# A two-layer hybrid block in float32: where the tiles begin in SBUF

## The chip, the cores and the metric

The kernel runs on one core of a Trainium2 chip. The metric is the device time of one execution in microseconds; the runs of the kernel before are given as a median with their lowest and highest. One further execution was taken with the hardware profiler, and all times of engines and instructions below are from that one.

## The reference

Two layers, each of a feed-forward half step, a mixer with three branches, and a second feed-forward half step, on 256 tokens of width 1024, in float32:

```python
for l in range(2):
    x = x + 0.5 * swiglu(rms_norm(x, ffn1_norm[l]), ffn1_w_gate[l], ffn1_w_up[l], ffn1_w_down[l])
    x = x + hybrid_mixer(rms_norm(x, mix_norm[l]), w_in[l], ..., w_branch[l], w_out[l])
    x = x + 0.5 * swiglu(rms_norm(x, ffn2_norm[l]), ffn2_w_gate[l], ffn2_w_up[l], ffn2_w_down[l])
```

swiglu(x) is (silu(x @ w_gate) * (x @ w_up)) @ w_down with 2816 hidden columns. hybrid_mixer projects its input with w_in and has three branches: a gated linear recurrence, a dilated window attention with 12 heads, and a chunked delta rule with 8 heads (a chain of small triangular solves). Their outputs go through w_branch, are gated, added, and go through w_out.

## The kernel before, in words

**The big matmuls.** Everything is kept transposed: features on the 128 partitions, the 256 tokens in the columns. A product with a weight matrix is a sum over blocks of 128 x 128 weights. Each float32 product is made of three products in the type float32r: a weight block w is split into wh (rounded) and wl (the rest), an activation into xh and xl, and wh xh, wh xl and wl xh are added up in PSUM. Two helpers issue them. In `stationary` the weight block is the stationary operand, loaded into TensorE by LDWEIGHTS, and the activation the moving one, 256 columns; this is nearly all of the kernel. In `moving`, used by the attention projections (kinds ak, aq, av), the activation is the stationary operand and the weight tile the moving one. Both call `pump` between matmuls, which may let another piece of work (a task) issue its instructions in between.

**The weights.** They lie in HBM in the order of use. `load_group` fetches one group of up to 1024 columns (512 KB) into one of the six tiles raw0 to raw5 through SyncE's queue; `convert` makes wh and wl of it, by ScalarE (rarely VectorE) and VectorE, in five tiles each of 1024 columns. A 128-column slice of such a tile is 512 bytes per partition.

**The small work.** Norms, gates, convolutions, the recurrence, the attention and the delta rule run as tasks (generators) on VectorE, ScalarE, GpSimd and, with small float32 matmuls into the PSUM tiles sm, on TensorE. Activations xh and xl live in 60 places s0 to s59 of 256 columns (1024 bytes per partition); larger ones in the arena, tiny ones in the tile tiny.

**What sets the order.** The whole order of instructions is fixed when the program is built. `Engine._cost` puts a price in ns on every instruction, `Prog.count` adds it to the planned clock of its engine, and `pump` issues a step of a task as soon as the planned clock of TensorE (`now`) has passed the planned end of what the step needs. The price of a float32r matmul is in `Engine._cost`: 0.46 ns for each moving column, so 117.8 ns for 256. A price does nothing on the chip; it decides behind which big matmul a step is issued. `move` chooses between ScalarE and VectorE by the same planned clocks.

**Where the tiles lie.** The pool sb places its tiles in SBUF one after another, in the order in which `Prog.__init__` declares them, each at a multiple of 32 bytes. cst (8280 bytes per partition) begins 128 bytes past a multiple of 1024, prm (1760) follows, then raw, wh, wl, X, zr, ssq, which all have sizes that are multiples of 1024 bytes and begin 960 bytes past such a multiple; eps_n and half (32 bytes each) fill the 64 bytes up to the next multiple, at which tiny begins, and so the arena and the places s behind it. Blocks within the arena begin at multiples of 256 bytes.

Of the kernel before, what the change touches and what calls it, by code (L numbers as in the profile page):

```python
# [10 lines left out]
F32 = mybir.dt.float32  # L11
# [6 lines left out]
P = 128  # L18
# [21 lines left out]
KEEP, KEEP2 = 3072, 2048  # L40
ARENA_COLS = 14336
NSLOT = 60
SPARE = 4
SLACK = (800.0, 1500.0, 1500.0, 1500.0, 1500.0, 600.0)
URGENT = 2
# [54 lines left out]
def flat_chunks():  # L100
    return [c for layer in all_jobs() for jobs in layer for job in jobs for c in job[2]]


def group_chunks(chunks):
    groups, cur, cols = [], [], 0
    for c in chunks:
        w = c[3] * c[5]
        if cur and cols + w > GROUP_COLS:
            groups.append((cur, cols))
            cur, cols = [], 0  # L110
        cur.append(c)
        cols += w
    groups.append((cur, cols))
    return groups
# [60 lines left out]
class Arena:  # L175
    def __init__(self, pr, ap, unit):
        self.pr, self.ap, self.unit = pr, ap, unit
        self.n = ap.shape[1] // unit
        self.busy = [False] * self.n
        self.stamp = [0.0] * self.n  # L180
        self.peak = 0
# [123 lines left out]
def _free(ap):  # L305
    n = 1
    for x in ap.shape[1:]:
        n *= x
    return n


class Engine:
# [16 lines left out]
    def _cost(self, name, a, k):  # L329
        key = self._key  # L330
        if key == "pe":
            lhsT = k["lhsT"] if name == "matmul" else a[1]
            rhs = k["rhs"] if name == "matmul" else a[2]
            n, m = _free(rhs), _free(lhsT)
            if lhsT.dtype == F32R:
                return max(0.46 * n, 0.83 * m)
            if name == "transpose":
                return 0.84 * max(n, m)
            if m <= 32 and lhsT.shape[0] <= 32:
                return 40.0  # L340
            if m <= 64 and lhsT.shape[0] <= 64 and n <= 64:
                return 100.0
            return 1.7 * max(n, m)
        n = _free(a[0])
        if name == "tensor_reduce":
            n = _free(a[1])
        if key == "a":
            c = 93 + 0.833 * n
            for x in ("scale", "bias", "accum_out"):
                c += 93 * (not isinstance(k.get(x, 0.0), float) and x in k)  # L350
            func = a[2] if name == "activation" else None
            sets = TABLES.get(func)
            if sets and self._pr.table not in sets:
                self._pr.table = sets[0]
                c += 1283
            return c
        if key == "g":
            return (330 + 160 * n) if k.get("op") == ALU.pow else 350 + 0.6 * n
        if name == "reciprocal":
            return 68 + 6.3 * n  # L360
        fast = name in ("tensor_copy", "tensor_scalar") and a[1].space != PSUM
        c = 68 + (0.52 if fast else 1.04) * n
        if name in ("scalar_tensor_tensor", "tensor_scalar") and not isinstance(a[2], float):
            c += 60
        if k.get("accum_out") is not None:
            c += 60
        return c
# [5 lines left out]
class Prog:  # L373
    def __init__(self, ctx, tc, io):
        self.tc, self.nc, self.io = tc, tc.nc, io
        nc = self.nc
        self.clock = {"pe": 0.0, "v": 0.0, "a": 0.0, "g": 0.0}
        self.table = None
        self.cur = self.main = Task(None, 0.0, 0)
        self.step, self.used = set(), {}  # L380
        self.tasks = []
        self.pe, self.v = Engine(self, "pe", nc.tensor), Engine(self, "v", nc.vector)
        self.a, self.g = Engine(self, "a", nc.scalar), Engine(self, "g", nc.gpsimd)
        sb = ctx.enter_context(tc.tile_pool(name="sb", bufs=1))
        ps = ctx.enter_context(tc.tile_pool(name="ps", bufs=1, space=PSUM))
        dr = ctx.enter_context(tc.tile_pool(name="dr", bufs=1, space=bass.MemoryType.DRAM))
        self.cst = sb.tile([P, CST["_n"]], F32, name="cst")
        self.prm = sb.tile([P, L * PRM["_n"]], F32, name="prm")
        self.raw = [sb.tile([P, GROUP_COLS], F32, name=f"raw{i}") for i in range(NRAW)]
        self.wh = [sb.tile([P, 1024], F32R, name=f"wh{i}") for i in range(NCONV)]  # L390
        self.wl = [sb.tile([P, 1024], F32R, name=f"wl{i}") for i in range(NCONV)]
        self.X = sb.tile([P, KD, T], F32, name="X")
        self.zr = sb.tile([P, T], F32, name="zr")
        self.ssq = sb.tile([P, T], F32, name="ssq")
        self.eps_n = sb.tile([P, 1], F32, name="eps_n")
        self.half = sb.tile([P, 8], F32, name="half")
        self.tiny_t = sb.tile([P, 1024], F32, name="tiny")
        self.ar_t = sb.tile([P, ARENA_COLS], F32, name="arena")
        self.tiny = Arena(self, self.tiny_t, 8)
        self.slots = Slots(self, sb, NSLOT)  # L400
        self.ar = Arena(self, self.ar_t, 64)
        self.big = Banks(self, [ps.tile([P, 512], F32, name=f"big{i}") for i in range(NBIG)])
        self.sm = Banks(self, [ps.tile([P, 512], F32, name=f"sm{i}") for i in range(8 - NBIG)])
        self.gdram = [dr.tile([16, P], F32, name=f"gd{l}") for l in range(L)]
        self.rdram = [[dr.tile([P, 64], F32, name=f"rd{l}_{i}") for i in range(4)] for l in range(L)]
        self.rc = [self.tiny.get(16).ap for _ in range(L)]
        self.ea = [self.tiny.get(8) for _ in range(L)]
        self.qg = [self.tiny.get(6) for _ in range(L)]
        self.groups = group_chunks(flat_chunks())
        self.chunk_at = []  # L410
        off = 0
        self.goff = []
        for gi, (cs, cols) in enumerate(self.groups):
            self.goff.append(off)
            c0 = 0
            for c in cs:
                self.chunk_at.append((c, gi, c0, c[3] * c[5]))
                c0 += c[3] * c[5]
            off += P * cols
        self.unread = [len(cs) for cs, _ in self.groups]  # L420
        self.cursor = 0
        self.dma_next = 0
        self.dma_clock = 0.0
        self.raw_t = {}
        self.conv_t = {}
        self.conv_next = 0
        self.when = {}
        self.ops = {}
        self.prepared = set()
        self.nsq = None  # L430
        self.npair = 4
# [111 lines left out]
    def get(self, cols):  # L543
        b = None
        if cols == T:
            b = self.slots.get(F32, SPARE)
        return b or self.ar.get(cols, self.keep())
# [1157 lines left out]
```

## Time and profile before

| | |
|---|---|
| runs of the kernel before | median 1630.62 us of 3 (1622.04 to 1631.97) |
| the profiled execution, its own time | 1627.63 us |
| its span, first to last instruction | 1625.4 us |
| mean granted clock of TensorE | 0.994 |
| TensorE matmuls busy | 1602.4 us |
| VectorE, ScalarE, GpSimd busy | 1159.2, 936.7, 139.3 us |
| read from HBM | 275.49 MB, 170 GB/s over the span |

The span is 2.2 us shorter than the execution's own time. In rows, PE is TensorE's matmuls, PEld its weight loads, DVE is VectorE, ACT ScalarE, POOL GpSimd. Nearly all instructions are issued from one line, that of the wrapper in class Engine (L323 before), so groups are told apart by the tiles: `big<-s,wh` is a matmul into a PSUM tile big with the moving operand s and the stationary operand wh; `128*128` is its rows and stationary columns, `128x256` what it writes; buffer numbers are left out. Matmuls are pipelined: a row's time in us reaches into the next row's, and what one matmul costs in a stream is the distance between starts.

### The profile page before, as it was taken

What the parts mean: (1) busy time and instruction counts of PE and PEld (TensorE: products, weight loads), DVE (VectorE), ACT (ScalarE), POOL (GpSimd) and SP (SyncE); (2) the same over time, 40 slices, a digit from 0 to 9 for tenths busy, and PEclk for the clock granted to TensorE, in tenths of its full rate; (3) what the DMA queues carried; (4) which work ended last, traced back from release to release, by engine and by line L of the source; (5) the groups of instructions that cost most, each with busy time, mean ns of one, the idle gap of its engine ahead of it and who ended that gap; (6) DMA issues with size and microseconds to landing.
All of it is one profiled execution on the core that took longest, in us unless ns stands there. A gap on an engine that the chain in (4) does not pass through costs nothing. (4 is left out here: it accounts for less than half of the span.)

```text
span 1625.4 us, 34428 instructions
## 1 busy us (share of the span) xinstructions
PE 1602.4 (99%) x13952; PEld 1560.0 (96%) x13952; DVE 1159.2 (71%) x2172; ACT 936.7 (58%) x1643; POOL 139.3 (9%) x280
## 2 busy tenths in 40 slices
PE   9999999999999999999999999999999999999999
PEld 8999999989988999999999999999898899999999
DVE  8666588987973667666566656989878756676653
ACT  7544456878854546444454445568887555554442
POOL 0000000345002000000000000003540120000000
PEclk9999999999998999999999999999999999999999
DMA  8655656544343565555555555656443345655562
GB/s 304 186 187 179 193 179 194 164 162 133 120 129 107 163 204 184 187 188 178 188 192 183 182 185 185 195 176 182 139 140 122 123 131 189 190 184 185 181 188 86
DMA packets 84942, 279.04 MB, mean 172 GB/s; under 512 B 10256, under 2 KB 15664, under 8 KB 84784
## 3 DMA queue, kind: packets, MB, share of 16 engines
q1 hardware_dynamic: 84784, 276.85, 53.7%
q8 instruction: 109, 1.79, 0.4%
q14 instruction: 49, 0.40, 0.1%
HBM read 275.49 MB, written 1.33 MB: 170 GB/s over the span
## 5 line engine op out<-in xcount | busy, mean ns | idle before, releaser
L323 PE MATMUL big<-s,wh 128*128 128x256 f32 (+1 forms) x7520 | 1346.3, 281 | 7.0 <-DVE s L323 6.0
L323 PEld LDWEIGHTS big<-s,wh 128*128 128x128 f32 (+1 forms) x7520 | 1151.0, 188 | 17.4 <-DVE s L323 6.8
L323 PE MATMUL big<-s,wl 128*128 128x256 f32 (+1 forms) x3760 | 1053.6, 280 | 0.0
L323 DVE TENSOR_TENSOR wl<-raw,wh 128x1024 fp32r<-128x1024 f32 (+3 forms) x523 | 620.8, 1187 | 248.4 <-ACT wh L323 245.2
L323 ACT ACTIVATE wh<-raw 128x1024 fp32r<-128x1024 f32 (+4 forms) x497 | 509.1, 1025 | 361.8 <-PE big L323 168.8
L323 PEld LDWEIGHTS big<-s,wl 128*128 128x128 f32 (+1 forms) x3760 | 705.3, 188 | 2.8 <-issue 1.8
L323 ACT ACTIVATE s<-s 128x256 fp32r<-128x256 f32 (+1 forms) x213 | 85.2, 413 | 116.6 <-DVE s L323 116.0
L323 POOL TENSOR_TENSOR tiny<-tiny,half 128x4 f32<-128x4 f32 (+1 forms) x28 | 38.6, 1378 | 1102.0 <-DVE tiny L323 1083.9
L323 PE MATMUL sm<-arena 128*128 128x128 f32 (+7 forms) x1440 | 114.0, 238 | 9.7 <-DVE arena L323 6.9
L323 PEld LDWEIGHTS sm<-arena 32*32 32x32 f32 (+5 forms) x1440 | 85.8, 138 | 30.2 <-issue 9.3
L323 PE MATMUL big<-wh,s 128*128 128x256 f32 x576 | 110.2, 287 | 0.0
L323 POOL TENSOR_TENSOR arena<-arena 128x60 f32<-128x60 f32 (+14 forms) x240 | 98.6, 411 | 62.6 <-DMA arena<-rd 44.7
L323 DVE TENSOR_TENSOR s<-s,s 128x256 fp32r<-128x256 f32 (+1 forms) x181 | 75.7, 422 | 36.5 <-ACT s L323 36.1
L323 PEld LDWEIGHTS big<-wh,s 128*128 128x128 f32 x576 | 89.6, 189 | 1.2
L323 DVE SCALAR_TENSOR_TENSOR s<-big,prm,s 128x255 f32<-128x255 f32 (+2 forms) x183 | 85.6, 477 | 6.6 <-ACT s L323 5.3
L323 DVE TENSOR_TENSOR arena<-big,zr 128x512 f32<-128x512 f32 x88 | 60.9, 692 | 34.8 <-PE big L323 34.5
L323 PE MATMUL big<-wl,s 128*128 128x256 f32 x288 | 82.1, 285 | 0.0
L323 ACT ACT_TABLE_LOAD x63 | 80.8, 1283 | 1.7 <-PEq L1697 0.7
L323 ACT ACTIVATE arena<-sm 128x128 f32<-128x128 f32 (+6 forms) x152 | 48.8, 323 | 37.6 <-PE sm L323 35.1
L323 ACT ACTIVATE s<-big 128x256 f32<-128x256 f32 x53 | 20.2, 382 | 62.1 <-PE big L323 62.1
L323 PEld LDWEIGHTS big<-wl,s 128*128 128x128 f32 x288 | 54.5, 189 | 0.4
L323 ACT ACTIVATE s<-big,prm 128x256 f32<-128x256 f32 x53 | 26.5, 499 | 45.2 <-PE big L323 45.0
(110 smaller groups left out, 772.3 us busy)
## 6 DMA issues: line engine op xcount, KB each, us to landing
raw<-wts SPq DMA_DIRECT2D x435, 512.0 KB, 3.7
raw<-wts SPq DMA_DIRECT2D x64, 448.0 KB, 3.6
raw<-wts SPq DMA_DIRECT2D x16, 384.0 KB, 3.1
arena<-rd SPq DMA_DIRECT2D x8, 512.0 KB
arena<-rgw SPq DMA_DIRECT2D x4, 512.0 KB, 5.2
arena<-gd SPq DMA_DIRECT2D x16, 128.0 KB, 4.7
X<-x SPq DMA_DIRECT2D x4, 256.0 KB, 4.9
raw<-wts SPq DMA_DIRECT2D x4, 256.0 KB, 3.2
```

Of the source, the lines that this page charges most:

```text
L323: r = f(*a, **k)
```

## The change

The constants tile eps_n and the tile half are declared right behind prm, and behind them a tile pad of 252 columns (1008 bytes) that nothing uses. eps_n and half now lie at 960 and 992 bytes past a multiple of 1024, the pad begins on the next multiple's place, and raw0 begins on a multiple of 1024; wh, wl, X, zr, ssq, tiny, the arena and the places s follow, all of them on multiples. In the built program raw0 goes from byte 26,560 to 27,648, wh0 from 51,136 to 52,224, s0 from 163,840 to 164,864. The second edit is the planner's price of a float32r matmul, 0.445 instead of 0.46 ns for a column.

```diff
@@ -40,6 +40,7 @@
 NSLOT = 60
+PAD = 252
 SPARE = 4
@@ -333,7 +334,7 @@
             if lhsT.dtype == F32R:
-                return max(0.46 * n, 0.83 * m)
+                return max(0.445 * n, 0.83 * m)
@@ -386,14 +387,15 @@
         self.cst = sb.tile([P, CST["_n"]], F32, name="cst")
         self.prm = sb.tile([P, L * PRM["_n"]], F32, name="prm")
+        self.eps_n = sb.tile([P, 1], F32, name="eps_n")
+        self.half = sb.tile([P, 8], F32, name="half")
+        sb.tile([P, PAD], F32, name="pad")
         self.raw = [sb.tile([P, GROUP_COLS], F32, name=f"raw{i}") for i in range(NRAW)]
         self.wh = [sb.tile([P, 1024], F32R, name=f"wh{i}") for i in range(NCONV)]
         self.wl = [sb.tile([P, 1024], F32R, name=f"wl{i}") for i in range(NCONV)]
         self.X = sb.tile([P, KD, T], F32, name="X")
         self.zr = sb.tile([P, T], F32, name="zr")
         self.ssq = sb.tile([P, T], F32, name="ssq")
-        self.eps_n = sb.tile([P, 1], F32, name="eps_n")
-        self.half = sb.tile([P, 8], F32, name="half")
         self.tiny_t = sb.tile([P, 1024], F32, name="tiny")
```

The new price moves steps of tasks to other places between the big matmuls. Of TensorE's 12,467 rows in the built program some 305 stand elsewhere; the big matmuls keep their order. The numbers behind the names in the next rows count the buffers in the order in which they are made and differ between the two programs; only the kinds of tiles and the shapes are to be compared.

The first place is TensorE at the end of the first feed-forward half step, where the small matmul for the next norm (sm from ssq) is issued. Before:

```order
L323 MATMUL big_91<-s_1708,wh_77 128x256
L323 MATMUL big_91<-s_1709,wh_77 128x256
L323 MATMUL sm_95<-ssq,cst 128x256
L323 MATMUL big_91<-s_1708,wl_82 128x256
L323 MATMUL big_91<-s_1789,wh_77 128x256
```

and now:

```order
L324 MATMUL big_92<-s_1710,wh_80 128x256
L324 MATMUL big_92<-s_1711,wh_80 128x256
L324 MATMUL big_92<-s_1710,wl_85 128x256
L324 MATMUL sm_96<-ssq,cst 128x256
L324 MATMUL big_92<-s_1791,wh_80 128x256
```

The small matmul stands one big matmul later; in the long feed-forward parts there are only such places. The second is TensorE in the attention projections of the first layer, among which the first pair of heads of the delta rule starts its chain of small products (sm from arena, 32x16, sixteen of them in a step). Before:

```order
L323 MATMUL big_92<-wh_77,s_2420 128x256
L323 MATMUL sm_95<-arena 32x16 x16
L323 MATMUL big_92<-wh_77,s_2450 128x256
L323 MATMUL big_92<-wl_82,s_2450 128x256
L323 MATMUL big_92<-wh_77,s_2451 128x256
L323 MATMUL big_92<-wh_73,s_2479 128x256
L323 MATMUL big_92<-wl_78,s_2479 128x256
L323 MATMUL sm_96<-arena 32x16 x16
```

and now, 69 rows further on:

```order
L324 MATMUL big_91<-wh_79,s_2403 128x256
L324 MATMUL sm_96<-arena 32x16 x16
L324 MATMUL big_91<-wh_79,s_2431 128x256
L324 MATMUL big_91<-wl_84,s_2431 128x256
L324 MATMUL big_91<-wh_79,s_2432 128x256
L324 MATMUL big_91<-wh_79,s_2455 128x256
L324 MATMUL big_91<-wl_84,s_2455 128x256
L324 MATMUL big_91<-wh_79,s_2456 128x256
L324 MATMUL big_91<-wh_80,s_2493 128x256
L324 MATMUL big_91<-wl_85,s_2493 128x256
L324 MATMUL sm_97<-arena 32x16 x16
```

Between the two steps stood five big matmuls and now stand eight; the chain starts later among the big matmuls.

## Rows read from the trace of the kernel before

**Rows 1.** The page's busy time by engine (share of the span, instructions), and the last link of the chain that ended last in order of time (start us, us, what).

```profile
PE 1602.4 (99%) x13952; PEld 1560.0 (96%) x13952; DVE 1159.2 (71%) x2172; ACT 936.7 (58%) x1643; POOL 139.3 (9%) x280
...
1438.51 183.51 PE big L323 x1558
```

**Rows 2.** The largest of TensorE's waits: who waited for whom, us in total, times, longest.

```profile
PE sm L323 <- DVE arena L323: 8.6, 8, 2.2
```

**Rows 3.** The page's groups of instructions that are big matmuls: line, engine, operation, tiles and count, then busy us, mean ns of one, idle time before them.

```profile
L323 PE MATMUL big<-s,wh 128*128 128x256 f32 (+1 forms) x7520 | 1346.3, 281 | 7.0 <-DVE s L323 6.0
L323 PE MATMUL big<-s,wl 128*128 128x256 f32 (+1 forms) x3760 | 1053.6, 280 | 0.0
L323 PE MATMUL big<-wh,s 128*128 128x256 f32 x576 | 110.2, 287 | 0.0
L323 PE MATMUL big<-wl,s 128*128 128x256 f32 x288 | 82.1, 285 | 0.0
```

**Rows 4.** TensorE in order of time at 700 us (start us, us, engine, line, instruction and count): the first and the last wl of four triples of two wh and one wl each.

```profile
700.08 0.28 PE L323 MATMUL big<-s,wl 128*128 128x256 f32 x1
...
701.49 0.28 PE L323 MATMUL big<-s,wl 128*128 128x256 f32 x1
```

**Rows 5.** The same view: what stands ahead of the stretch from 540 us, four triples in it at 600 us (first and last wl), and what ends it.

```profile
539.95 0.60 PE L323 MATMUL sm<-cst,arena 128*128 128x128 f32 x4
...
600.01 0.28 PE L323 MATMUL big<-s,wl 128*128 128x256 f32 x1
...
601.37 0.28 PE L323 MATMUL big<-s,wl 128*128 128x256 f32 x1
...
634.99 0.59 PE L323 MATMUL sm<-ssq,cst 128*128 128x256 f32 x2
```

**Rows 6.** Busy time by stretch (from:to and its length in us; busy us and instructions of each engine; granted clock, share of the DMA engines, GB/s): first of the instructions that write or read a big tile alone, then of all.

```profile
16.00:290.00 274.00, 270.51 (x2284) 269.06 (x2282) 44.92 (x88) 9.19 (x19) 1.00 0.61 196
290.00:325.00 35.00, 31.19 (x251) 30.22 (x252) 12.32 (x27) 3.28 (x7) 1.00 0.53 165
410.00:540.00 130.00, 87.22 (x662) 80.27 (x662) 13.51 (x30) 6.34 (x17) 0.95 0.38 119
540.00:635.00 95.00, 94.37 (x827) 93.84 (x826) 9.29 (x22) 5.05 (x14) 1.00 0.61 196
635.00:1098.00 463.00, 459.30 (x3879) 457.30 (x3877) 63.45 (x118) 9.19 (x19) 1.00 0.58 185
1098.00:1133.00 35.00, 31.08 (x250) 30.11 (x251) 12.95 (x28) 3.27 (x7) 1.00 0.61 180
1218.00:1345.00 127.00, 94.29 (x707) 86.08 (x708) 12.68 (x29) 7.69 (x19) 1.00 0.40 126
1345.00:1626.00 281.00, 276.68 (x2342) 275.87 (x2340) 27.48 (x51) 4.61 (x12) 1.00 0.55 172
...
16.00:290.00 274.00, 273.83 (x2309) 272.08 (x2308) 203.40 (x369) 150.12 (x226) 1.01 (x1) 1.00 0.61 196
290.00:540.00 250.00, 241.23 (x2237) 224.00 (x2236) 190.21 (x478) 174.60 (x385) 68.45 (x137) 0.97 0.43 133
635.00:1098.00 463.00, 462.68 (x3907) 460.65 (x3906) 321.14 (x487) 241.74 (x355) 1.01 (x1) 1.00 0.58 185
1098.00:1345.00 247.00, 240.76 (x2284) 224.82 (x2283) 192.03 (x478) 177.88 (x391) 68.60 (x137) 1.00 0.45 140
```

**Rows 7.** A stretch with a lower granted clock (columns as in rows 6), and TensorE in order of time around it.

```profile
367.20:367.90 0.70, 0.70 (x6) 0.70 (x5) 0.70 (x5) 0.70 (x4) 0.00 (x0) 0.50 0.38 146
...
367.38 0.41 PE L323 MATMUL big<-wl,s 128*128 128x256 f32 x1
367.59 0.63 PE L323 MATMUL big<-wh,s 128*128 128x256 f32 x2
```

**Rows 8.** TensorE in order of time in two runs of the moving form: the first and last wl of one with 12 triples of matmuls between them, and of one with 15.

```profile
358.46 0.28 PE L323 MATMUL big<-wl,s 128*128 128x256 f32 x1
...
362.70 0.28 PE L323 MATMUL big<-wl,s 128*128 128x256 f32 x1
...
394.98 0.28 PE L323 MATMUL big<-wl,s 128*128 128x256 f32 x1
...
400.08 0.28 PE L323 MATMUL big<-wl,s 128*128 128x256 f32 x1
```

**Rows 9.** TensorE in order of time: float32 matmuls of 256 columns, several in a row (each is one pass of two).

```profile
289.70 0.81 PE L323 MATMUL sm<-s,arena 128*128 128x256 f32 x3
...
298.04 1.02 PE L323 MATMUL sm<-s,arena 128*128 128x256 f32 x4
...
1009.74 0.59 PE L323 MATMUL sm<-ssq,cst 128*128 128x256 f32 x2
```

**Rows 10.** Groups by form: VectorE additions and ScalarE activations of 128x256 with operands in ssq, X and the places s (count, busy us, mean ns of one, idle before).

```profile
L323 DVE TENSOR_TENSOR s<-s,s 128x256 f32<-128x256 f32 x62 | 25.8, 421 | 0.4
L323 DVE TENSOR_TENSOR ssq<-ssq,s 128x256 f32<-128x256 f32 x39 | 16.3, 418 | 0.2
L323 ACT ACTIVATE s<-s 128x256 f32<-128x256 f32 x85 | 32.4, 409 | 1.3 <-DVE s L323 0.8
L323 ACT ACTIVATE s<-X 128x256 f32<-128x256 f32 x39 | 15.6, 402 | 0.0
```

## The prediction

> **What bounds the kernel now.** I read the engine summary first, then the chain that ended last, then the table by stretch, and only then single matmuls. The summary shows TensorE busy for 1602.4 us of the span of 1625.4, and the last link of the chain is 183.51 us of nothing but big matmuls [rows 1]. That leaves 23 us of idle time, and the largest single kind of wait in it is 8.6 us [rows 2]. So time can only come from the matmuls themselves or from those few waits. The instruction groups show what they are: 7520 + 3760 with a weight tile as the stationary operand and an activation place as the moving one (I call this the stationary form), and 576 + 288 the other way round (the moving form, in the attention projections), 12,144 in all, each 256 columns wide [rows 3].
>
> A busy TensorE is not yet one at its peak, so the next thing to read is the spacing of starts. The chain gives it at once: 183.51 us / 1558 = 117.8 ns per matmul. The timeline gives the same at 700 us: four triples of matmuls, wh twice and wl once, in 1.41 us, 0.353 us each [rows 4]. But between 540 and 635 us four triples take 1.36 us, 0.340 each, which is 113.3 ns for a matmul [rows 5]. The clock is granted in full in both. So there are two spacings, fast and slow, 4.45 ns apart, and almost the whole kernel runs at the slow one: the table by stretch shows 8505 big matmuls in the stretches 16 to 290, 635 to 1098 and 1345 to 1626 us, where I find not one fast spacing, and 827 in the fast stretch [rows 6]. Layer 2's twin of the fast stretch (from 1345 us) is slow, with the same tiles and lines.
>
> **How the two spacings arise, as far as the trace tells.** A stream keeps its spacing until something else interrupts it: the fast stretch begins just behind four small matmuls at 539.95 us and ends behind two others at 634.99 us [rows 5]. Within a stream neither the slice of the weight tile nor the activation place matters; what differs is how the stream was entered. [...]
>
> Does the place of the weights matter for the entry? The declarations of the kernel before put raw, wh, wl, X, zr and ssq 960 bytes past a multiple of 1024 (64 bytes short of the next), and tiny, the arena and the places s on a multiple. So the two forms are an experiment that the kernel before makes by itself. In the stationary form the weight load reads from 960 or 448 and the moving read from 0; in the moving form the weight load reads an s place, from 0 or 512, and the moving read is the one off the multiple. Going through TensorE's timeline, I took each run of at least four big matmuls without an interruption: in the stationary form 76 of 82 runs end slow, in the moving form 33 of 49 end fast. A fast and a slow run of the moving form are shown [rows 8]; streams that follow small matmuls of the same kind are slow in the one form and often fast in the other. That points to the weight load's start, not to the moving operand's.
>
> **The change part by part.**
> 1. wh and wl begin at a multiple of 1024, so that in the stationary form the weight load starts at 0 or 512, as it does today only in the moving form. [...] I take 113.3 ns, the spacing that rows show for this very form and for weight loads from 0 and 512. The sum: 8505 matmuls x 4.45 ns = 37.8 us in the three long stretches, where nothing else holds TensorE (it is busy 273.83 of 274 and 462.68 of 463 us) [rows 6].
> 2. The mixer stretches: in 290 to 325, 410 to 540, 1098 to 1133 and 1218 to 1345 us there are 251 + 662 + 250 + 707 = 1870 matmuls of the stationary form [rows 6], 8.3 us at 4.45 ns. Here TensorE already stands still for 8.8 us of 250 and 6.2 of 247, and VectorE and ScalarE are at 70 to 78% [rows 6]. The big matmuls fill the time of a chain of small ones; a shorter filler is partly waited out. I count half, 4.2 us, bounds 0 and 8.3. The moving form in 325 to 410 and 1133 to 1218 us is two thirds fast already, by the runs told of above: nothing counted.
> 3. The other engines' reads and writes of raw, wh, wl, X and ssq. VectorE takes 418 ns for ssq<-ssq,s and 421 for s<-s,s, ScalarE 402 from X and 409 from s [rows 10]: on or off the multiple is the same. Nothing counted. VectorE is 69 to 74% busy in the first two long stretches [rows 6]; a 4% faster TensorE takes it to 72 to 77%, and TensorE's wait on it stays rare. The weights land well ahead: in the fast stretch TensorE never waited for a DMA, at 0.61 of the DMA engines' time [rows 6].
> 4. The planner's price for a big matmul falls from 0.46 x 256 = 117.8 to 0.445 x 256 = 113.9 ns. It moves no work out of or into TensorE: 305 of its 12,467 rows stand elsewhere, in the long stretches a single small matmul each (the first place shown in the section on the change), in the mixer whole steps of a chain (the second place). Fourteen operations pass from VectorE to ScalarE, hidden behind TensorE. What the order is worth shows in TensorE's idle time in the mixer, 15 us in both layers: I take 0, bounds -7.5 (half of the waits go) and +7.5 (half as much again).
> 5. eps_n, half and the pad are moved addresses without work: 0.
>
> Sum against the profiled execution's 1627.63 us: 37.8 + 4.2 = 42.0, so 1585.6, rounded 1586 us. The median of the runs shown is 1630.62. The lottery of the spacings explains that spread: the profiled run has its one long fast stretch, 827 x 4.45 = 3.7 us; without it, it would be 1631.3, near the two highest runs.
>
> [...]
>
> **The rivals.**
> - Nothing changes (the price moves a few rows). For it: the state is set by the entry, the same places ran fast in layer 1 and slow in layer 2, and a float32 pass more costs 0.21 us whether the moving tile is s, at 0 (1.02 us for four, 0.81 for three), or ssq, at 960 (0.59 for two, 0.38 for one by the two others) [rows 9]. Against it: 76 of 82 against 33 of 49. It gives 1627.6, from 1622 to 1635 with the lottery and the order.
> - A mixed state: the entry stays a matter of chance, two thirds fast as in the moving form today. 42 x 2/3 = 28 us, so 1600; with one third to five sixths, 1593 to 1614.
> - Slower: with both operands on the same multiple, the weight load and the moving read, today 64 bytes apart, could meet at every matmul. Price: another excess of 4.45 ns on top of the slow spacing over 12,144 matmuls, 54 us, 1682 us. It decides from 119.1 ns on (16.3 us / 12,144 = 1.3 ns above 117.8). Against it: the arena and s share a multiple today, and their float32 passes show no excess [rows 9], though at half the rate.
> - Better than fast: both on the multiple bring it below 113.3. [...] Against it: the fast spacing is the same whichever operand lies off the multiple [rows 5, 8].
>
> **How the numbers follow.** All or nearly all fast 0.50 (own range 1574 to 1594: the bounds of steps 2 and 4), mixed 0.20, nothing 0.17, slower 0.08, better 0.05. A measurement of this kernel can tell about 1%, 16 us, from no change; faster by more than that is the first, most of the mixed and the last case, 0.72; within it 0.18; slower 0.10, with a small share for an unlucky order. The range from 1574 to 1632 leaves out the better and the worse case and a part of the third.
>
> **What would show it.** In the changed profile, three big matmuls in 0.340 us in the long stretches, so some 882 instead of 849 in 100 us, with clock, instruction count and the other engines' durations as before; the chain's last link near 1558 x 113.3 = 176.5 us. Step 2 is wrong if TensorE's idle time in the mixer grows by more than 8 us, step 4 if it grows with the spacing unchanged. The forecast is wrong if the long stretches still show 0.353 us.

## The result and the profile after

The changed kernel takes 1650.37 us, median of 4 runs (1648.12 to 1651.39); the kernel before, run beside it, 1631.30 (1622.04 to 1632.39). The ratio is 1.0117 [1.0094 to 1.0139]: the change costs 1.2%. The prediction, 1586 us and faster, was wrong in size and in sign. The profiled execution took 1651.13 us with a span of 1648.0, 22.6 us longer than before, at a granted clock of 0.998 against 0.994 before, so the clock explains none of the loss.

The page of the changed kernel, busy time by engine, and the last link of the chain that ended last (start us, us, what), as in [rows 1]:

```profile
PE 1630.2 (99%) x13952; PEld 1586.5 (96%) x13952; DVE 1151.6 (70%) x2157; ACT 938.8 (57%) x1657; POOL 141.3 (9%) x280
...
1457.76 186.84 PE big L324 x1557
```

The number of matmuls is the same, 13,952, and the busy time of TensorE grew by 27.8 us. The last link says what one matmul costs now: 186.84 / 1557 = 120.0 ns, against 117.8 before. TensorE in order of time at 700 us (start us, us, instruction), the wl of four triples:

```profile
700.18 0.28 PE L324 MATMUL big<-s,wl 128*128 128x256 f32 x1
...
700.54 0.28 PE L324 MATMUL big<-s,wl 128*128 128x256 f32 x1
...
700.90 0.28 PE L324 MATMUL big<-s,wl 128*128 128x256 f32 x1
...
701.26 0.28 PE L324 MATMUL big<-s,wl 128*128 128x256 f32 x1
```

Three triples in 1.08 us, 0.360 each; before it was 0.353 [rows 4], and 0.340 in the fast stretch [rows 5]. The groups of big matmuls (columns as in [rows 3]):

```profile
L324 PE MATMUL big<-s,wh 128*128 128x256 f32 (+1 forms) x7520 | 1376.6, 284 | 7.3 <-DVE s L324 4.6
L324 PE MATMUL big<-s,wl 128*128 128x256 f32 (+1 forms) x3760 | 1067.5, 284 | 0.0
L324 PE MATMUL big<-wh,s 128*128 128x256 f32 x576 | 113.5, 291 | 0.0
L324 PE MATMUL big<-wl,s 128*128 128x256 f32 x288 | 83.3, 289 | 0.0
```

The mean time of one row is 3 to 4 ns longer in both forms, in the moving form too; a row reaches into the next one, so what a matmul costs more is read from the starts, 2.2 ns. By stretch (columns as in [rows 6]), first of the instructions at a big tile, then of all:

```profile
16.00:290.00 274.00, 272.70 (x2267) 271.83 (x2266) 43.54 (x84) 9.19 (x20) 1.00 0.60 194
640.00:1105.00 465.00, 463.13 (x3847) 461.64 (x3846) 62.63 (x115) 9.50 (x20) 1.00 0.58 183
1355.00:1648.00 293.00, 286.94 (x2370) 284.91 (x2369) 27.88 (x52) 4.97 (x13) 1.00 0.53 167
...
290.00:540.00 250.00, 247.41 (x2306) 230.65 (x2305) 193.44 (x494) 180.50 (x398) 68.20 (x137) 1.00 0.46 140
1105.00:1355.00 250.00, 243.77 (x2247) 226.35 (x2246) 191.68 (x492) 171.96 (x379) 70.84 (x137) 0.99 0.44 135
```

In the 274 us from 16 to 290 the view counts 2267 big matmuls, where it counted 2284. TensorE does not wait more: in the mixer it stands still for 2.6 of 250 and 6.2 of 250 us, less than the 8.8 of 250 and 6.2 of 247 before. Its two largest waits (who waited for whom, us, times, longest) are small:

```profile
PE big L324 <- DVE s L324: 4.6, 9, 1.5
PE sm L324 <- DVE tiny L324: 4.0, 3, 1.5
```

And the other engines' instructions cost what they did (columns as in [rows 10]):

```profile
L324 DVE TENSOR_TENSOR ssq<-ssq,s 128x256 f32<-128x256 f32 x39 | 16.3, 418 | 0.2
L324 DVE TENSOR_TENSOR s<-s,s 128x256 f32<-128x256 f32 x64 | 26.5, 423 | 0.3
L324 ACT ACTIVATE s<-X 128x256 f32<-128x256 f32 x39 | 15.6, 402 | 0.0
```

So most of the time went into the spacing of big matmuls. Summed over all distances between starts, what follows a big matmul went from 1469.7 to 1501.1 us (+31.4) and what follows a small one from 150.8 to 142.0 (-8.8); together that is the 22.6 us. Most of the first sum comes out of counts: before, of 11,742 spacings in streams, 1276 were at 113.3 and 10,466 at 117.8; now 10,407 of the stationary and 535 of the moving form are at 120, and some 600 still at 117 to 119. With all of them at 120 it would be 10,466 x 2.2 + 1276 x 6.7 = 31.6 us, and those 600 take off some 1.3. That this is so near 31.4 is partly luck: the spacings of up to 125 ns between two big matmuls are worth 25.7 us of the sum, with 37 fewer of them, and the longer ones 6.1 us.

### The profile page after: what moved, and what is told of

Read it like the earlier page. It is cut to its first block, busy times and chain, and to the rows that moved or that the text cites. A ratio compares the mean times of both kernels' runs of the same rounds, so it can differ in the third digit from the quotient of the medians.

```text
span 1648.0 us, 34442 instructions
## 1 busy us (share of the span) xinstructions
PE 1630.2 (99%) x13952; PEld 1586.5 (96%) x13952; DVE 1151.6 (70%) x2157; ACT 938.8 (57%) x1657; POOL 141.3 (9%) x280
## 5 line engine op out<-in xcount | busy, mean ns | idle before, releaser
L324 PE MATMUL big<-s,wh 128*128 128x256 f32 (+1 forms) x7520 | 1376.6, 284 | 7.3 <-DVE s L324 4.6
L324 PEld LDWEIGHTS big<-s,wh 128*128 128x128 f32 (+1 forms) x7520 | 1174.8, 191 | 20.3 <-DVE s L324 8.8
L324 PE MATMUL big<-s,wl 128*128 128x256 f32 (+1 forms) x3760 | 1067.5, 284 | 0.0
L324 ACT ACTIVATE wh<-raw 128x1024 fp32r<-128x1024 f32 (+3 forms) x496 | 509.0, 1026 | 479.4 <-issue 264.1
L324 PEld LDWEIGHTS big<-s,wl 128*128 128x128 f32 (+1 forms) x3760 | 720.1, 192 | 3.5 <-issue 2.9
L324 PE MATMUL sm<-arena 16*32 16x16 f32 (+8 forms) x1424 | 110.2, 234 | 4.9 <-DVE tiny L324 4.0
L324 PE MATMUL big<-wh,s 128*128 128x256 f32 x576 | 113.5, 291 | 0.0
L324 PEld LDWEIGHTS sm<-arena 32*32 32x32 f32 (+5 forms) x1424 | 82.5, 134 | 23.6 <-issue 8.7
L324 DVE SCALAR_TENSOR_TENSOR s<-big,prm,s 128x255 f32<-128x255 f32 (+2 forms) x174 | 82.1, 478 | 14.7 <-ACT s L324 13.3
```

The lines of the kernel that those rows point to most:

```text
L324: r = f(*a, **k)
```

## The experiments

Below, distance is the place of the weight load's operand minus that of the moving one, modulo 256 bytes. Before, it is 960 - 0, which is 192 or -64, in the stationary form, and +64 in the moving form; after the change it is 0 in both. In the chains quoted, the link is always the last stream of big matmuls (start us, us, what). Kernels that ran side by side share their runs of the kernel before.

**Which of the two edits.** e1_price is the kernel before with the new price alone:

```diff
-                return max(0.46 * n, 0.83 * m)
+                return max(0.445 * n, 0.83 * m)
```

> The tiles stay where they were before (weights 960 bytes past a multiple of 1024, places s on a multiple), the planner's price is the new one, 0.445. Theory A, the place of the weights alone sets the new spacing of 120.0 ns: the spacing stays at 117.8 and 113.3 ns and the time at that of the kernel before, 1622 to 1635 us. Theory B, the order that the new price makes (the way streams are entered) is what changed the spacing: 120.0 ns and about 1650 us here too.

e2_places is the changed kernel with the old price:

```diff
-                return max(0.445 * n, 0.83 * m)
+                return max(0.46 * n, 0.83 * m)
```

> The tiles lie as in the changed kernel, all on multiples of 1024, with the old price 0.46 and so the order of before. Theory A (the places): 120.0 ns in nearly all big matmuls, 12,144 x 2.2 to 2.4 ns above before, 1645 to 1655 us. Theory B (the order): 117.8 ns and 1622 to 1635 us.

Measured: e1_price 1624.00 us (10 runs) against 1627.43 (13 runs), ratio 0.9978 [0.9965 to 0.9992]; e2_places 1653.27 (4 runs), 1.0163 [1.0145 to 1.018]. The links of e1_price and of e2_places:

```profile
1437.41 183.39 PE big L323 x1557
```

```profile
1461.95 186.96 PE big L324 x1558
```

117.8 ns with the old places, 120.0 with the new ones. The places cost 1.6% alone; the price gives back 0.2%, a gain within the bounds set for it. Together that is 1.4%, just above the interval measured for both edits (1.2%). It is also the price's order that shortens the time after small matmuls: 142.9 us in e1_price, 149.0 in e2_places, 150.8 before. Most of that is no gain: in e1_price the time after big matmuls is 6.7 us longer than before (1476.4 against 1469.7), and the span of its profile only 1.2 us shorter (1624.2). The new order goes with a higher granted clock, too: 0.996 to 0.999 in the ten runs of e1_price, 0.993 to 0.996 in the 13 of the kernel before. How much of the 0.2% that is was not separated.

**Own place or distance.** e3_both960 leaves the weights at 960 and moves the places s there too:

```diff
+        sb.tile([P, 240], F32, name="pad")
         self.tiny_t = sb.tile([P, 1024], F32, name="tiny")
```

> The kernel before with one pad of 960 bytes behind half, so that tiny, the arena and the places s begin 960 bytes past a multiple of 1024, as the weights do. The weight load and the moving read are again at distance 0, but neither lies on a multiple. Theory A1, the distance between the two operands' places counts: 120.0 ns and about 1650 us. Theory A2, the place of each for itself counts (being on a multiple of 128 or more): 117.8 or 113.3 ns, 1580 to 1635 us.

Measured: 1651.41 us (one run), and the link

```profile
1458.85 186.96 PE big L323 x1558
```

again 120.0 ns. The weights' place is that of the kernel before, the moving operand's is new, and the result is that of the changed kernel, where it is the other way round. What the two share is the distance 0.

**The map.** m1_map is a program of its own: streams of 48 big matmuls of the kernel's shape, no other engine at work beside them, over 6 places of the moving operand (ma 0, mb 64, mc 128, md 256, me 512, mf 960) and 10 of the weights (wa 0, wb 32, wc 64, wd 96, we 128, wf 192, wg 256, wh 320, wi 384, wj 448; v lies as w), each pair entered behind three kinds of small matmuls.

> Only the matmuls, no block: streams of 48 float32r matmuls of the stationary form (wh, wh, wl), three streams for each pair of places, entered behind two float32 matmuls of 128 columns, eight of 16 columns, or one of 256; the weights 0, 32, 64, 96, 128, 192, 256, 320, 384 or 448 bytes past a multiple of 512 (tiles wa to wj with va to vj), the moving tile 0, 64, 128, 256, 512 or 960 past a multiple of 1024 (ma to mf); the output is the input x. Theory A1 (distance): the spacing depends on weights minus moving place modulo 512 alone; 120.0 ns at 0, 117.8 or 113.3 at -64, 113.3 at +64, so the same pattern comes back shifted with the moving place. Theory A2 (each place for itself): the spacing depends on the weights' column alone, 120.0 at 0 for all moving places. Theory C (only the entry counts): no pattern by place, but one by the kind of entry.

Measured: 1135.11 us in all. TensorE in order of time: the v of pair ma,wa; of ma,wf in its first and its second stream; of mc,we; of mc,wf; of mf,wf (the rows between are left out):

```profile
22.00 0.28 PE L70 MATMUL big<-ma,va 128*128 128x256 f32 x1
...
23.44 0.28 PE L70 MATMUL big<-ma,va 128*128 128x256 f32 x1
...
108.57 0.28 PE L70 MATMUL big<-ma,vf 128*128 128x256 f32 x1
...
111.75 0.28 PE L70 MATMUL big<-ma,vf 128*128 128x256 f32 x1
...
116.01 0.28 PE L70 MATMUL big<-ma,vf 128*128 128x256 f32 x1
...
117.37 0.28 PE L70 MATMUL big<-ma,vf 128*128 128x256 f32 x1
...
463.73 0.28 PE L70 MATMUL big<-mc,ve 128*128 128x256 f32 x1
...
465.17 0.28 PE L70 MATMUL big<-mc,ve 128*128 128x256 f32 x1
...
481.89 0.28 PE L70 MATMUL big<-mc,vf 128*128 128x256 f32 x1
...
483.25 0.28 PE L70 MATMUL big<-mc,vf 128*128 128x256 f32 x1
...
1041.82 0.28 PE L70 MATMUL big<-mf,vf 128*128 128x256 f32 x1
...
1043.26 0.28 PE L70 MATMUL big<-mf,vf 128*128 128x256 f32 x1
```

Twelve matmuls take 1.44 us (120.0 ns) where both operands start alike modulo 256, be it at 0, at 128, or at 960 and 192. For ma,wf, the pair of the kernel before, one stream runs at 3.18 / 27 = 117.8 and one at 1.36 / 12 = 113.3: the two spacings of [rows 4, 5], for the same instructions and addresses, with VectorE and ScalarE busy for 0.00 us and the DMA engines at a share of 0.00 from 60 to 1130 us. For mc,wf 12 take 1.36 us. The mean spacing in ns by distance, for each of the three streams:

```
distance     moving 0            moving 64           moving 128          moving 960
   0      120.0/120.0/120.0   120.0/120.0/120.0   120.0/120.0/120.0   120.0/120.0/120.0
 +64      117.8/113.4/117.7   113.3/113.4/117.8   113.4/113.3/113.3   113.4/113.4/117.8
+128      118.5/118.5/118.4   118.7/118.8/118.9   118.7/118.5/118.4   118.6/118.6/118.4
 -64      117.8/113.4/117.7   117.8/117.8/117.8   117.8/117.8/117.7   113.3/117.7/117.7
```

Weights 256 bytes further give the same three numbers but for two first streams (moving 64, weights 384: 117.8; moving 960, weights 320: 120.0), and moving places 256 and 512 give the column of 0. Distance 0 has one spacing and the worst of these four; +64 and -64 have 113.3 and 117.8, and at +64 the lower comes more often.

**The distance turned round.** The map points to the moving operand at 128 and the weights at 192, which asks for a pad of 128 bytes. e4_s128 is the kernel before with this line; e6_s128_price adds the new price to it; e5_w64 reaches distance +64 from the other side, weights at 64 and s at 0 (the changed kernel with PAD 268, a second pad of 240 columns ahead of tiny, and the old price).

```diff
+        sb.tile([P, 32], F32, name="pad")
         self.tiny_t = sb.tile([P, 1024], F32, name="tiny")
```

> The kernel before with one pad of 128 bytes behind half: weights stay 960 past a multiple of 1024 (192 past one of 256), tiny, the arena and the places s begin 128 past a multiple of 256; old price. Weights minus moving place is now +64 modulo 256, before -64. Theory A1 (distance, as the map shows it: all six streams with m at 128 and weights at 192 or 448 were at 113.3 ns): the stationary form runs at 113.3 ns, 8505 + 1870 matmuls x 4.45 ns less, 1580 to 1592 us. Theory A1' (distance +64 and -64 are alike, the entry decides): a mixture of 113.3 and 117.8 ns, 1595 to 1630 us.

> The same places with the new price 0.445, which now agrees with the spacing on the chip if that is 113.3 ns. Theory A1: 1576 to 1592 us, at most 4 us better than with the old price, as with the old places (0.22% there). If a price that agrees with the chip mattered much, over 8 us better.

> Weights, raw, X, zr and ssq 64 past a multiple of 1024, tiny, the arena and the places s on a multiple; old price. Distance +64 with the moving operand at 0, where the map showed one stream in three at 113.3 ns and two at 117.8. By the map a mixture, 1590 to 1630 us; if the sign of the distance alone decided, all fast, 1580 to 1592 us; if +64 is like -64, 1622 to 1632 us. In no case 120 ns.

Measured: e4_s128 1594.47 us (1590.90 to 1603.86, 4 runs) against 1628.88, ratio 0.9805 [0.977 to 0.9839]; e6_s128_price 1607.42 (1591.59 to 1614.54, 4 runs), 0.989 [0.9849 to 0.9931]; e5_w64 1602.21 (one run). e4_s128 beats both kernels: its page, its link, and four triples at 700 us:

```profile
PE 1566.7 (98%) x13952; PEld 1524.1 (96%) x13952; DVE 1157.3 (73%) x2172; ACT 936.4 (59%) x1643; POOL 139.5 (9%) x280
...
1410.65 176.60 PE big L323 x1558
```

```profile
699.96 0.28 PE L323 MATMUL big<-s,wl 128*128 128x256 f32 x1
...
701.32 0.28 PE L323 MATMUL big<-s,wl 128*128 128x256 f32 x1
```

The link is at 176.60 / 1558 = 113.35 ns, the triples at 0.340 us. Of its big spacings 9418 are fast and 2324 slow, 1276 and 10,466 before. The time lies between the two expected ranges. The map had all three streams of this pair fast; in the kernel some 53 of 85 runs of the stationary form are, so the map's three streams do not stand for all of the kernel's. The moving form, now at -64, has turned over: 42 of 48 runs slow, where 33 of 49 were fast. e6_s128_price shows that the price's 0.2% does not add up: it is no faster than e4_s128, above its expected range, and its runs spread over 23 us. Its profiled run, the fastest of the four, has 8334 fast spacings; the other three have no trace, so that the spread is one of streams that came out slow is likely and not shown. e5_w64 has 7202 fast and 4542 slow, a mixture, as the map has one for moving 0.

**Finer places.** m2_fine is the map in steps of 16 bytes of the weights, for eight moving places 32 bytes apart. e7_m96 (weights 160, s 96), e8_m160 (224, 160) and e9_m32 (weights 192, s 224, distance -32) are kernels out of it, by pads ahead of raw and of tiny.

```diff
-WOFF = (0, 32, 64, 96, 128, 192, 256, 320, 384, 448)
-MOFF = (0, 64, 128, 256, 512, 960)
+WOFF = tuple(range(0, 256, 16))
+MOFF = tuple(range(0, 256, 32))
```

> Only streams of 24 float32r matmuls of the stationary form behind the same three kinds of entry; weights 0 to 240 past a multiple of 256 in steps of 16 (tiles wa to wp with va to vp), the moving tile 0 to 224 in steps of 32 (ma to mh); the output is the input x. Theory A1: the pattern depends on the distance modulo 256 and shifts with the moving place: 120.0 ns at 0 for each moving place, two spacings (113.3 and 117.8) at 64 and 192, 118.5 at 128. Theory A2 (place for itself): the columns alone. What a distance that is no multiple of 64 gives is open; if it always gave 113.3 ns or less, that would be the place to choose.

```diff
+        sb.tile([P, 56], F32, name="padw")     # e7_m96; 8 in e8_m160; none in e9_m32
         self.raw = [sb.tile([P, GROUP_COLS], F32, name=f"raw{i}") for i in range(NRAW)]
...
+        sb.tile([P, 32], F32, name="pads")     # e7_m96 and e8_m160; 56 in e9_m32
         self.tiny_t = sb.tile([P, 1024], F32, name="tiny")
```

> Weights 160 and the places s 96 past a multiple of 256, distance +64 as with 192 and 128; old price and order. The fine map showed all three streams at 113.3 ns for the pairs (96, 160), (128, 192) and (160, 224), and one or two of three for the other pairs at +64. If the place itself decides how surely a stream becomes fast, all three pairs behave alike and this run has the time of the pair (128, 192), 1585 to 1605 us. If it is the chance of the entry alone, anything from 1585 to 1610 us with another split between 113.3 and 117.8 ns.

> Weights 224 and the places s 160 past a multiple of 256, distance +64; old price and order. As for the pair (96, 160): 1585 to 1605 us; a pair that is faster by over 8 us than the others would show that the place itself counts beside the distance.

> Weights 192 and the places s 224 past a multiple of 256, distance -32 (224): the fine map shows 116.4 to 116.8 ns there for nearly all moving places and entries, no second spacing. If the map of bare matmuls carries over to the kernel by distance alone: 116.5 ns in the stationary form, some 1.3 ns x 10,500 = 14 us below a kernel that is all slow (1631), 1612 to 1622 us, and little spread between runs. If the bistable pair 113.3 and 117.8 appears instead, the map does not carry over.

Measured: the fine map (1323.19 us) has 120.0 ns at distance 0 for all eight moving places at a granted clock of 1.0, nothing below 113.3, three fast streams of three only at +64 with the moving operand at 96, 128 or 160, and 116.7 in all streams but one at -32 (117.8). Distance 0 is not alone at the slow end: +112 and -96 are at 120 in every stream, -16, -112, +96 and others in some, and at +48 three streams of 24 are at 123.3. So more distances than two have several spacings. Nor do place and kind of entry settle which one comes: moving 0 with weights 64 has 117.8 ns in its first stream in the first map and 113.3 in this one. TensorE in order of time (the v of ma,wo, moving 0 and weights 224; of me,wm, moving 128 and weights 192):

```profile
159.89 0.28 PE L71 MATMUL big<-ma,vo 128*128 128x256 f32 x1
...
161.29 0.28 PE L71 MATMUL big<-ma,vo 128*128 128x256 f32 x1
...
791.69 0.28 PE L71 MATMUL big<-me,vm 128*128 128x256 f32 x1
...
793.05 0.28 PE L71 MATMUL big<-me,vm 128*128 128x256 f32 x1
```

Twelve matmuls take 1.40 us (116.7 ns) at -32 and 1.36 (113.3) at +64. e7_m96 took 1613.71 us (4 runs) against 1631.75, 0.9898 [0.9868 to 0.9927]; e8_m160 1606.03 (4 runs), 0.9855 [0.9803 to 0.9907]; e9_m32 1621.18 (8 runs), 0.9945 [0.9928 to 0.9962]. The links of e7_m96 and e9_m32:

```profile
1423.66 183.51 PE big L323 x1558
```

```profile
1436.41 181.78 PE big L323 x1558
```

e7_m96 and e8_m160 gain, but less than expected (1585 to 1605): a last stream at 117.8 in both, and 4857 and 5393 fast spacings, show that the pair being fast in all three streams of the map does not make it so in the kernel. Whether 128 is a better place than 96 and 160, or e4_s128 has luckier entries, is not settled; they ran on different chips. e9_m32's time, just inside the range, and its link (181.78 / 1558 = 116.7 ns) are as expected. Its profile also has some 2120 spacings at 113.3 and 2180 at 120, but these are no streams of their own: in most of its long streams the distances between starts go 113, 116, 118 and 120 ns in turn, and bare streams of the fine map at -32 show the same cycle; others go 116, 117, 117. Both have the mean 116.7. At this distance the map carries over to the kernel.

**Other shapes.** m3_shape keeps the moving operand at 128 and changes the columns of both operands, for five places of the weights (wa 128, wb 192, wc 0, wd 64, we 96; v lies as w).

```diff
-WOFF = (0, 32, 64, 96, 128, 192, 256, 320, 384, 448)
-MOFF = (0, 64, 128, 256, 512, 960)
+WOFF = (128, 192, 0, 64, 96)
+MOFF = (128,)
+FORMS = ((256, 128), (512, 128), (256, 128), (128, 128), (512, 64), (256, 64))
```

> Only streams of 24 float32r matmuls, the moving tile 128 past a multiple of 256, the weights at distance 0, 64, 128, 192 and 224 (tiles wa to we), behind the three kinds of entry; moving columns 512, 256 and 128 with 128 stationary columns, and 512 and 256 with 64; the output is the input x. [...] Theory A4, the moving read is slower for each column: it doubles with 512 columns, 240.0 and 226.7 ns, and does not care for the stationary columns.

Measured: 397.49 us in all; TensorE in order of time, 512 columns at distance 0 and at +64, then 128 columns at distance 0:

```profile
65.11 0.39 PE L69 MATMUL big<-ma,va 128*128 128x512 f32 x1
...
68.51 0.39 PE L69 MATMUL big<-ma,va 128*128 128x512 f32 x1
...
81.84 0.39 PE L69 MATMUL big<-ma,vb 128*128 128x512 f32 x1
...
84.64 0.39 PE L69 MATMUL big<-ma,vb 128*128 128x512 f32 x1
...
206.07 0.27 PE L69 MATMUL big<-ma,va 128*128 128x128 f32 x1
...
207.41 0.27 PE L69 MATMUL big<-ma,va 128*128 128x128 f32 x1
```

15 matmuls in 3.40 us (226.7 ns), 12 in 2.80 (233.3), 12 in 1.34 (111.7). In ns:

```
moving columns / stationary   dist. 0   +64     +128    -64     -32
512 / 128                      226.7    233.3   232.9   228.9   233.3
256 / 128                      120.0    113.3   118.8   117.8   116.7
128 / 128                      111.7    111.7   111.7   111.7   111.7
512 / 64                       230.0    232.0   229.2   228.3   230.7
256 / 64                       113.3    119.0   116.7   116.7   118.8
```

The distance matters at both widths above 128 columns, by up to 6.7 ns, but the best one belongs to one shape: with 512 moving and 128 stationary columns distance 0 is the best of the five and +64 the worst, together with -32; with 256 and 64 it is 0 against +64 again; with 512 and 64 -64 is the best (each row is of one moving place; the first stream of 256 / 64 at +128 is at 120.0). With 128 stationary columns, going from 256 to 512 moving columns adds 106.7 ns at distance 0 and 120.0 at +64, so that no one price for a column holds at both. Theory A4 asked for twice the spacings of 256 columns, 240.0 and 226.7 ns at the two distances, and neither came; nor do the stationary columns leave it alone, as it had it: with 64 of them 256 moving columns take 113.3 and 119.0 ns there, with 128 of them 120.0 and 113.3.

## Why the prediction was wrong

**What bounds the kernel: right.** TensorE's spacing is the time, by [rows 1 to 4] and in the changed kernel too: the other engines' instructions cost what they did, TensorE does not wait more, and most of the added time is that of the spacings.

**Step 1, the failing step.** It read 76 of 82 slow runs in the stationary form and 33 of 49 fast ones in the moving form (80 of 84 and 33 of 47 if runs of five or more are counted) as "That points to the weight load's start, not to the moving operand's." On this rests its term of 37.8 us. The two forms differ in the weight load's place, but in the sign of the distance between the two operands too, and the evidence could not separate them. It is the distance: with the weights left at 960 a spacing of 120.0 appears as soon as the moving operand comes to 960 as well (e3_both960), and in the map 120.0 goes with distance 0 and with no place of one operand alone. (Which of its spacings a stream takes at 64 either way is another matter, see below.) The rows for "weight loads from 0" all had the moving read 64 bytes off; the change took that away along with the weights' offset. Where 8505 matmuls of the long stretches were to gain 4.45 ns each, 37.8 us, nearly all of them lost 2.2 ns, some 18.7 us; over all of the kernel the time after big matmuls grew by 31.4 us, and by 28.7 with the places alone (e2_places).

**The rival "slower".** It had the condition that counts, both operands on the same multiple, with a chance of 0.08. Its point of decision (119.1 ns) was passed, and its price of 4.45 ns was twice the measured 2.2. That the two reads "could meet at every matmul" is its reason; no run shows what meets, and +112 and -96 are at 120 ns too. What was held against it, that float32 passes with both operands on one multiple show no excess [rows 9], where a pass more takes 0.21 us with s as with ssq, was a case at about half the data rate (256 columns in 0.21 us against 117.8 ns) and says nothing of the full one. "Better" asked for less than 113.3 ns; no stream of 256 columns in the maps is below that.

**The entry as a lottery: right for the streams, not shown for the spread of runs.** The map shows it bare: at -64 and +64 one pair has both spacings. At distance 0 there is no such choice, and the changed kernel's four runs lie within 3.3 us, those of the kernel before within 10.4. But e7_m96, at +64 with both spacings in its profile, has its four runs within 2.8 us, so a small spread alone says little.

**Steps 2 and 3.** No gain in the mixer, since its matmuls became slower too; TensorE's idle time there did not grow. Step 3 is right: 418 ns for ssq, 421 to 423 for s, 402 from X, whatever the place.

**Step 4.** Taken at 0 with bounds of 7.5 us either way; measured a gain of 3.4 us (e1_price, 0.9978 [0.9965 to 0.9992]). Step 5 costs nothing that any row shows. The range given for "all fast" ends too low by its own bounds: 1585.6 + 4.2 + 7.5 is 1597, not 1594; nothing here hangs on it.

What stays open: why the spacing goes by the distance modulo 256, why some streams fall to 113.3 and others to 117.8, and by which rule the best distance goes with the shape.

## What to carry to other kernels

Where TensorE streams float32r matmuls without a gap, read the spacing of starts from the timeline, vary the distance of the two operands' starts modulo 256 bytes with a pad of a few columns, in the kernel's own shape, and measure again: here one pad of 128 bytes was worth 2.0% with one order of instructions and 1.1% with another, and round multiples for all cost 1.2%. When two forms of an instruction differ in more than one respect, what tells them apart in a trace is not yet known; one run that changes one respect costs less than the argument.

## What was not expected of the hardware

- The spacing of 128x256 float32r matmuls goes by the distance of the two operands modulo 256 bytes: 120.0 ns at 0, 118.5 at 128, 116.7 at -32, and 113.3 or 117.8 at 64 either way. A mean can hide a cycle: at -32 most streams take 113, 116, 118 and 120 ns in turn.
- At a distance of 64 a stream keeps the one of two spacings that it fell into, as the links of 1558 matmuls show, at 113.35 ns in e4_s128 and at 117.8 in the kernel before. The runs of one kernel at such a distance can lie 23 us apart (e6_s128_price, 1591.59 to 1614.54); that the streams are the reason is likely and not shown.
- 128 moving columns take 111.7 ns at each of the five distances, almost as long as 256 at their fastest (113.3). What sets the pace there no run separates.
- The spacings lie in steps near 6.7 ns (113.3, 120.0; 226.7, 233.3) besides values between them, and of distances 0 and +64, the better one of 256 moving and 128 stationary columns is the worse one with 512 columns or 64 stationary ones.
